# MLP up product by Strassen's seven products, hidden rows through DRAM, down product contraction-outermost

## The chip, the cores and the metric

The kernel runs on one core of a Trainium2 chip. The metric is the device time of one execution in microseconds; a profiled execution is taken beside it. Engines are named as in the profile: PE (TensorE, matmuls; PEld its weight loads), DVE (VectorE), ACT (ScalarE), POOL (GpSimd) and SP (SyncE, which issues the DMAs of this kernel). 

## The reference

One decoder layer over 1024 tokens with model width 1024. A normalised input is projected for three mixers (a gated convolution, a state-space scan, a windowed attention), which are gated, summed and projected back; then comes a cross-attention over 256 memory tokens, and then the MLP. What the change touches is the end:

```
h = h + CrossAttn(RMSNorm(h), RMSNorm(mem))       # ends with a product by w_xo, 1024 x 1024
u = RMSNorm(h)                                    # gain g_mlp per channel, 1/rms per token
h = h + relu(u @ w_mlp_up)**2 @ w_mlp_down        # 1024 -> 4096 -> 1024
```

All data are float32.

## The kernel before

Activations lie with channels on the 128 partitions and the 1024 tokens along the free side: a tile `ht[i]` is 128 channels x 1024 tokens, eight of them are the residual stream h.

Every product is made from split operands. A float32 tile is cut into a rounded part (`oh`, `wh`, a copy by ACT into the fp32r type) and the rest (`ol`, `wl`, a subtraction by DVE for activations, by POOL for weights). A product is then three matmuls, high x high, high x low, low x high, added up in PSUM. A matmul has 128 x 128 weights and 512 tokens. `gemm_ch` makes one output tile of 128 x 1024 in a pair of PSUM banks (pool `pg`, two such tiles): 6 matmuls for each 128 channels of contraction, so 48 for a contraction of 1024 and 24 for one of 512. Pool `pss` has four more banks, and the eight banks are then all used. `wslot` loads 128 x 1024 weights from DRAM by SP's queue into a staging tile (`wst`, two), and splits them by ACT (L155) and POOL (L156) into `wp` (three pairs).

The kernel is written in a tile framework: a tool orders the instructions by priorities and readiness and puts in the semaphores. Code inside `high_priority` (the weight loads) goes ahead of its place in the text. `after(n, fn)` lays small pieces of work n steps later between the matmuls of a product; `step()` counts these, and `drain()` runs what is left. `token_rstd` sums squares over channels by small matmuls and makes 1/rms per token; `spread` multiplies it into a diagonal and makes a tile of it, equal on all partitions, by four matmul records (`ps_bs`).

The end of the cross-attention: `project` (L1291) takes the heads in two halves of the contraction, each 8 outputs of 24 matmuls. DVE adds the result to `ht[i]` (L1298). In the second half, `done(i)` (L1317) also splits ht[i] with the gain g_mlp on it (ACT L1054, DVE L1055), squares it (ACT L1322) and sums the squares (POOL L1323). So the MLP multiplies un-normalised activations, and 1/rms comes in afterwards, because it is one number per token.

The MLP (L1334 to L1357) goes over eight blocks. A block makes four hidden tiles (`gemm_ch` with contraction 1024, 48 matmuls each). DVE takes the positive part times 1/rms out of PSUM (L1345), ACT squares (L1346) and rounds (L1051), DVE takes the difference (L1052). The four hidden tiles are then multiplied by `w_down` (contraction 512): eight outputs of 24 matmuls, each added by DVE to `ht` (L1355). In the last block the sums are stored (L1357).

The stage that follows the attention, `branch(load_split(...))` (L1069 to L1105), is the one place where a product's activations are loaded from DRAM and split (`yin`, L1076).

Of the kernel before, what the change touches and what calls it, by code (L numbers as in the profile page):

```python
# [9 lines left out]
F32 = mybir.dt.float32  # L10
F32R = mybir.dt.float32r
AF = mybir.ActivationFunctionType
# [43 lines left out]
def trunk_kernel(tc, w_io):  # L56
# [3 lines left out]
    with ctx:  # L60
# [26 lines left out]
        def after(n, fn):  # L87
            side.append((steps_done[0] + n, fn))
# [14 lines left out]
        def drain():  # L103
            while side:
                side.pop(0)[1]()
# [28 lines left out]
        d_v = dram.tile([NT, P, 256], F32, name="d_v")  # L134
        d_z = dram.tile([16, P, T], F32, name="d_z")
        d_cs = dram.tile([8, 32, P], F32, name="d_cs")
        d_bv = dram.tile([16, 384], F32, name="d_bv")
        d_skew = dram.tile([16, P * 385], F32, name="d_skew")

        def wslot(src, first=False, pool_=None, stage=None):  # L140
            with ExitStack() as e:
                if not first:
                    e.enter_context(tc.high_priority())
                st = (stage or wst).tile([P, 1024], F32, tag="ws", name="ws", bufs=2 if stage else None)
                if isinstance(src, list):
                    for n, part in enumerate(src):
                        nc.sync.dma_start(
                            st.rearrange("p (k n c) -> p k n c", k=2, n=2)[:, :, n, :],
                            part.rearrange("p (k c) -> p k c", c=256),
                        )  # L150
                else:
                    nc.sync.dma_start(st, src)
                wh = (pool_ or wp).tile([P, 1024], F32R, tag="wh", name="wh")
                wl = (pool_ or wp).tile([P, 1024], F32R, tag="wl", name="wl")
# [1030 lines left out]
        with ExitStack() as sc:  # L1185
# [102 lines left out]
                ):  # L1288
                    after(start + at, lambda fn=fn, args=args: fn(*args))

            def project(hh, parts, done):  # L1291
                for i2 in range(4):
                    wh, wl = wslot(w_io["w_xo"][hh, i2])
                    for j in range(2):
                        cols = lambda w, k: w[:, k * 256 + j * P:k * 256 + j * P + P]
                        ps = gemm_ch(lambda k: (cols(wh, k), cols(wl, k)), hi(parts), lo(parts), 4, T)
                        hv = ht[i2 * 2 + j]
                        dve.tensor_add(hv, hv, ps)  # L1298
                        done(i2 * 2 + j)

            parts0 = [pair(opb) for _ in range(4)]
            qT = queries(0)
            qT1 = queries(1)
# [7 lines left out]
            project(0, parts0, lambda i: None)  # L1311
            drain()
            both = q2.tile([P, 2, T], F32, tag="xqT", name="sq2")
            acc = both[:, 0, :]
            u3 = []

            def done(i):  # L1317
                u3.append(split(opc if i < 4 else opb, ht[i], C("g_mlp", i)))
                if i == 0:
                    act.activation(acc, ht[i], AF.Square)  # L1320
                else:
                    act.activation(both[:, 1, :], ht[i], AF.Square)  # L1322
                    pool.tensor_add(acc, acc, both[:, 1, :])  # L1323
            project(1, parts1, done)
            rb = xr.tile([P, T], F32, tag="acc", name="rb")
            dg = q2.tile([P, 2, T], F32, tag="xqT", name="hm_dg")
            r = []
            after(4, lambda: r.append(token_rstd(xr, acc, T, 1.0 / D, EPS, "hm")))
            after(6, lambda: spread(xr, r[0], T, "hm", rb, dg[:, 0, :]))
            up0 = gemm_ch(ch_slots(w_io["w_up"][0]), hi(u3), lo(u3), KT, T)  # L1330
            drain()


        with ExitStack() as sc:  # L1334
            ope = sc.enter_context(tc.tile_pool(name="ope", bufs=2))
            rt = sc.enter_context(tc.tile_pool(name="rt", bufs=2))
            n = 0
            for blk in range(8):
                parts = []
                for i in range(4):  # L1340
                    ps = up0
                    if blk or i:
                        ps = gemm_ch(ch_slots(w_io["w_up"][blk * 4 + i]), hi(u3), lo(u3), KT, T)
                    r = rt.tile([P, T], F32, tag="relu", name="relu")
                    dve.scalar_tensor_tensor(r, ps, 0.0, rb, ALU.max, ALU.mult)  # L1345
                    act.activation(r, r, AF.Square)  # L1346
                    parts.append(split(opa if n % 6 < 4 else ope, r))
                    n += 1
                for i2 in range(4):
                    wh, wl = wslot(w_io["w_down"][blk, i2])  # L1350
                    for j in range(2):
                        cols = lambda w, k: w[:, k * 256 + j * P:k * 256 + j * P + P]
                        ps = gemm_ch(lambda k: (cols(wh, k), cols(wl, k)), hi(parts), lo(parts), 4, T)
                        hv = ht[i2 * 2 + j]
                        dve.tensor_add(hv, hv, ps)  # L1355
                        if blk == 7:
                            nc.sync.dma_start(w_io["outT"][i2 * 2 + j], hv)  # L1357


# [105 lines left out]
```

## Time and profile before

| what | before |
|---|---|
| time, median of 3 runs | 2794.09 us (2794.03 to 2796.2) |
| time of the profiled execution | 2794.76 us |
| its span, first to last instruction | 2793.0 us |
| mean granted TensorE clock | 0.994 |
| PE / DVE / ACT / POOL busy, share of the span | 98% / 51% / 36% / 30% |
| matmul records | 12892 |
| moved by DMA | 267 MB, mean 96 GB/s |

A page of the profile gives the busy time of each engine, the same in 40 slices, the chain of work that ended last, and the costliest groups of instructions. A group's line has the line of the kernel, the engine, the operation, output<-inputs, partitions x elements, count, busy time, mean duration, and how long the engine stood idle before it and for whom. The trace behind it can be asked for a stretch, a line or a tile.

### The profile page before, as it was taken

To read this page: it belongs to the slowest core of one execution; us is meant where nothing else is said; L and a number is where in the kernel's file an instruction comes from. 1 tells how busy PE (TensorE), PEld (TensorE's weight loads), DVE (VectorE), ACT (ScalarE), POOL (GpSimd) and SP (SyncE) were. 2 spreads that over 40 slices of the span, in tenths; PEclk is the share of its full clock that TensorE was granted. 3 is DMA by queue.
4 is the path that set the end of the run, shared out by engine and by line. 5 is a ranking of instruction groups with operands and counts; after the bars stand their busy time and mean duration, and the time that the engine had idled before them with its cause. 6 is when DMAs were issued, how large, how long until landed. Compare 5 with 4: busy or idle time off the path is not lost. (4 is left out here: it accounts for less than half of the span.)

```text
span 2793.0 us, 31816 instructions
## 1 busy us (share of the span) xinstructions
PE 2737.7 (98%) x12892; PEld 2211.6 (79%) x12892; DVE 1430.1 (51%) x1610; ACT 1005.0 (36%) x1662; POOL 839.4 (30%) x376
## 2 busy tenths in 40 slices
PE   8899999999999999999899999999999999999999
PEld 6688878887787878765588778898778888888887
DVE  7578878759777876634414675223342222222222
ACT  6523321213565555556511352245432211122111
POOL 4622222201626252434242522420142222222221
PEclk9999999999999999999999999999999999999999
DMA  6552332321333233442444332310111111111111
GB/s 230 178 143 95 100 119 86 112 101 43 114 113 116 98 122 111 166 144 88 148 166 142 113 106 89 107 54 27 50 38 46 53 46 46 53 46 46 53 46 76
DMA packets 94515, 267.22 MB, mean 96 GB/s; under 512 B 9104, under 2 KB 34080, under 8 KB 93984
## 3 DMA queue, kind: packets, MB, share of 16 engines
q1 hardware_dynamic: 94368, 265.19, 28.6%
q8 instruction: 101, 1.65, 0.2%
q14 instruction: 46, 0.38, 0.0%
HBM read 210.47 MB, written 57.83 MB: 96 GB/s over the span
## 5 line engine op out<-in xcount | busy, mean ns | idle before, releaser
L156 POOL TENSOR_TENSOR wl<-ws,wh 128x1024 fp32r<-128x1024 f32 x200 | 500.7, 2506 | 1360.8 <-ACT wh L155 1330.9
L73 PE MATMUL ps_g<-oh,wh 128*128 128x512 f32 x1792 | 562.8, 395 | 4.1 <-ACT oh L1051 4.1
L73 PE MATMUL ps_g<-ol,wh 128*128 128x512 f32 x1792 | 555.6, 391 | 3.9 <-DVE ol L1052 3.4
L73 PE MATMUL ps_g<-oh,wl 128*128 128x512 f32 x1792 | 553.7, 390 | 0.0
L155 ACT CAST wh<-ws 128x1024 fp32r<-128x1024 f32 x200 | 209.7, 1049 | 869.6 <-PE ps_g L73 779.2
L332 DVE SCALAR_TENSOR_TENSOR tapy<-hin,cst,tapy 128x1024 f32<-128x1024 f32 x240 | 389.9, 1625 | 31.0 <-ACT tapy L327 24.7
L73 PEld LDWEIGHTS ps_g<-oh,wh 128*128 128x128 f32 x1792 | 335.6, 188 | 81.1 <-issue 7.1
L73 PEld LDWEIGHTS ps_g<-ol,wh 128*128 128x128 f32 x1792 | 335.8, 188 | 80.4 <-DVE ol L1052 9.7
L73 PEld LDWEIGHTS ps_g<-oh,wl 128*128 128x128 f32 x1792 | 336.9, 188 | 72.0
L73 PE MATMUL ps_g<-uh,wh 128*128 128x512 f32 x1008 | 330.6, 407 | 11.5 <-ACT uh L351 11.5
L73 PE MATMUL ps_g<-ul,wh 128*128 128x512 f32 x1008 | 324.4, 396 | 0.3 <-DVE ul L352 0.3
L73 PE MATMUL ps_g<-uh,wl 128*128 128x512 f32 x1008 | 315.7, 392 | 0.3 <-POOL wl L156 0.3
L73 PEld LDWEIGHTS ps_g<-ul,wh 128*128 128x128 f32 x1008 | 190.1, 189 | 50.0 <-issue 9.3
L73 PEld LDWEIGHTS ps_g<-uh,wl 128*128 128x128 f32 x1008 | 190.0, 189 | 41.7 <-POOL wl L156 1.2
L73 PEld LDWEIGHTS ps_g<-uh,wh 128*128 128x128 f32 x1008 | 178.9, 190 | 39.7 <-ACT uh L351 11.5
L1355 DVE TENSOR_TENSOR ht<-ht,ps_g 128x1024 f32<-128x1024 f32 x64 | 78.2, 1221 | 250.3 <-PE ps_g L73 250.3
L73 PE MATMUL ps_tm<-wh,uh 128*128 128x512 f32 x448 | 175.6, 392 | 0.0
L73 PE MATMUL ps_tm<-wh,ul 128*128 128x512 f32 x448 | 174.5, 389 | 0.0
L73 PE MATMUL ps_tm<-wl,uh 128*128 128x512 f32 x448 | 174.3, 389 | 0.0
L1345 DVE SCALAR_TENSOR_TENSOR relu<-ps_g,rb 128x1024 f32<-128x1024 f32 x32 | 39.2, 1225 | 221.8 <-PE ps_g L73 221.8
L170 POOL TENSOR_TENSOR wl<-ws,wh 128x1024 fp32r<-128x1024 f32 x28 | 74.9, 2685 | 218.5 <-ACT wh L169 218.5
L742 DVE SCALAR_TENSOR_TENSOR c4a<-c4v,cst,c4a 128x1023 f32<-128x1023 f32 (+2 forms) x72 | 98.7, 1370 | 32.0 <-ACT c4a L740 30.8
(341 smaller groups left out, 3417.3 us busy)
## 6 DMA issues: line engine op xcount, KB each, us to landing
ws<-w_ch SPq DMA_DIRECT2D x64, 512.0 KB, 3.5
csb<-d_cs SPq DMA_DIRECT2D x32, 512.0 KB, 4.0
gth<-d_th SPq DMA_DIRECT2D x32, 512.0 KB, 4.4
ws<-w_up SPq DMA_DIRECT2D x32, 512.0 KB, 3.3
ws<-w_down SPq DMA_DIRECT2D x32, 512.0 KB, 3.3
d_th<-gate_th SPq DMA_DIRECT2D x21, 512.0 KB, 5.1
ws<-w_xkv SPq DMA_DIRECT2D x32, 256.0 KB, 3.1
ws<-w_z SPq DMA_DIRECT2D x16, 512.0 KB, 3.3
```

The lines of the kernel that those rows point to most:

```text
L73: ins = nc.tensor.matmul(*a, **k)
L155: act.copy(wh, st)
L156: pool.tensor_sub(wl, st, wh.bitcast(F32))
L170: pool.tensor_sub(wl[:, :, c], s3, wh[:, :, c].bitcast(F32))
L332: dve.scalar_tensor_tensor(y, hin[:, j:j + T], w(j), y, ALU.mult, ALU.add)
L742: dve.scalar_tensor_tensor(a[:, s:], v[:, :T - s], C("c4_w", ct * 4 + 3 - s), a[:, s:], ALU.mult, ALU.add)
L1345: dve.scalar_tensor_tensor(r, ps, 0.0, rb, ALU.max, ALU.mult)
L1355: dve.tensor_add(hv, hv, ps)
```

## The change

In the projection's second half, 1/rms of the cross-attention's norm (already known) is spread over the partitions and multiplied into the MLP's input together with the gain. The outputs are made in the order 0, 4, 1, 5, 2, 6, 3, 7, so that each step has one tile of the upper and one of the lower half of the contraction. With tokens cut in two halves, the input is a 2 x 2 block matrix, and DVE makes the seven moving operands of Strassen's scheme (Winograd's form) from it: x11, x21, x22, t1 to t4, four tiles each, every one split in high and low part (`slice_of`). They fill the pools `opc`, `opb`, `opd` and the place of `ht` itself; h goes to DRAM (`d_h`).

The up product takes hidden tiles in 16 pairs. DVE makes the sums of weight blocks (s1, s2, s3 and one more), ACT and POOL split seven stationary operands per pair, PE makes seven products of 12 matmuls, each in one bank of `pss`, and DVE combines the results, takes relu and square in one operation, and SP stores them (`d_r`). ACT copies the first product out of PSUM.

The down product makes four output tiles at a time, in all eight PSUM banks, with the hidden rows outermost: each hidden tile is loaded from `d_r`, split, and multiplied into four outputs (24 matmuls); after 32 hidden tiles the outputs are multiplied by a per-token factor, added to h (loaded from `d_h`) and stored. This is done twice. The factor is the square of the ratio of the MLP norm's 1/rms to the one used on the input, made during the up product (`factor`).

```diff
-        def wslot(src, first=False, pool_=None, stage=None):
+        def wslot(src, first=False, pool_=None, stage=None, tags=("wh", "wl")):
...
+        def slice_of(name, src):
+            pool_, tag = next(spares)
+            t = pool_.tile([P, 2, 512], F32R, tag=tag, name="blk")
+            act.copy(t[:, 0, :], src)
+            dve.tensor_sub(t[:, 1, :], src, t[:, 0, :].bitcast(F32))
+            blocks.setdefault(name, []).append(t)
...
+            after(0, lambda: spread(xr, rx[0], T, "hx", rbx, dg))
+            for kp in range(4):
+                if kp % 2 == 0:
+                    slots = [wslot(w_io["w_xo"][1, kp // 2 + 2 * q]) for q in range(2)]
+                vs = []
+                for q in range(2):
+                    i = kp + 4 * q
+                    project(parts1, slots[q], i // 2, kp % 2)
+                    nc.sync.dma_start(d_h[i], ht[i])
+                    v = tp.tile([P, T], F32, tag="v", name="v")
+                    dve.scalar_tensor_tensor(v, ht[i], C("g_mlp", i), rbx, ALU.mult, ALU.mult)
...
+                        act.activation(sq, ht[i], AF.Square)
+                        pool.tensor_add(acc, acc, sq)
+                    lo_, hi_ = v[:, :512], v[:, 512:]
+                    if q == 0:
+                        slice_of("x11", lo_)
+                        t1 = tp.tile([P, 512], F32, tag="t1", name="t1", bufs=1)
+                        dve.tensor_sub(t1, hi_, lo_)
+                        slice_of("t1", t1)
+                t2, t3 = (tp.tile([P, 512], F32, tag="t", name="t") for _ in range(2))
+                b12, (b21, b22) = vs[0][:, 512:], (vs[1][:, :512], vs[1][:, 512:])
+                dve.tensor_sub(t2, b22, t1)
+                slice_of("t2", t2)
+                slice_of("x21", b21)
+                slice_of("x22", b22)
+                dve.tensor_sub(t3, b22, b12)
+                slice_of("t3", t3)
+                dve.tensor_sub(t2, b21, t2)
+                slice_of("t4", t2)
...
+            ORDER = (6, 1, 5, 7, 2, 3, 4)
+            for pr in range(16):
+                order = ORDER if pr else (1, 5, 6, 2, 3, 7, 4)
+                with tc.high_priority():
...
+                        w = (wst if q else mp).tile([P, 1024], F32, tag="ws", name="ws", bufs=2)
+                        nc.sync.dma_start(w, w_io["w_up"][pr * 2 + q])
...
+                    dve.tensor_add(s1, a21, a22)
+                    dve.tensor_sub(s2, s1, a11)
+                    dve.tensor_sub(s3, a11, a21)
...
+                            st[j] = stationary(srcs[j])
...
+                def square(o):
+                    dve.scalar_tensor_tensor(o, o, 0.0, o, ALU.max, ALU.mult)
+
+                for j in order:
+                    ps = banks[j] = pss.tile([P, 512], F32, tag="s", name="ps_up")
+                    for k in range(4):
+                        x = blocks[names[j]][k]
+                        wh, wl = (st[j][:, h, k * P:(k + 1) * P] for h in range(2))
+                        pe.matmul(ps, wh, x[:, 0, :], start=k == 0, stop=False)
+                        pe.matmul(ps, wh, x[:, 1, :], start=False, stop=False)
+                        pe.matmul(ps, wl, x[:, 0, :], start=False, stop=k == 3)
...
+                    if j == 1:
+                        act.copy(p1, ps)
+                    if j in (1, 6) and {1, 6} <= seen:
+                        dve.tensor_add(u2, p1, banks[6])
+                    if j in (5, 6) and {5, 6} <= seen:
+                        dve.tensor_add(u5, u2, banks[5])
+                    if j == 7:
+                        dve.tensor_add(u2, u2, ps)
+                        o = rb_[:, 512:]
+                        dve.tensor_add(o, u2, banks[5])
+                        square(o)
...
+                        nc.sync.dma_start(d_r[pr * 2 + 1], rb_)
...
+            for hf in range(2):
...
+                    for k in range(4):
+                        n = blk * 4 + k
+                        r = opc.tile([P, T], F32, tag="ol", name="r_in")
+                        nc.sync.dma_start(r, d_r[n])
...
+                        xh, xl = split(opb, r)
+                        for q in range(4):
...
+                            for h in range(2):
+                                sl = slice(h * 512, h * 512 + 512)
+                                pe.matmul(outs[q][h], wh, xh[:, sl], start=n == 0, stop=False)
+                                pe.matmul(outs[q][h], wh, xl[:, sl], start=False, stop=False)
+                                pe.matmul(outs[q][h], wl, xh[:, sl], start=False, stop=n == 31)
...
+                                    dve.tensor_mul(o[:, sl], outs[q][h], f[0][:, sl])
+                                    if hf:
+                                        dve.tensor_add(o[:, sl], o[:, sl], hs[q][:, sl])
+                                        nc.sync.dma_start(w_io["outT"][i][:, sl], o[:, sl])
...
+                                    pool.tensor_add(o, o, hs[q])
```

A stationary operand of an up pair (`stationary`) is split by an ACT copy and a POOL subtraction of 512 elements each, and there are ten buffers for them (three pairs of `wp`, four of `opa`).

## Rows read from the trace of the kernel before

**Rows 1.** The page: busy time and share of the span of each engine; the busy tenths of PE in 40 slices; the granted clock in tenths.

```profile
PE 2737.7 (98%) x12892; PEld 2211.6 (79%) x12892; DVE 1430.1 (51%) x1610; ACT 1005.0 (36%) x1662; POOL 839.4 (30%) x376
...
PE   8899999999999999999899999999999999999999
...
PEclk9999999999999999999999999999999999999999
```

**Rows 2.** Busy time by stretch: the second half of the projection, and the MLP from its first to its last matmul. Columns: stretch, its length, busy us (count) of PE, PEld, DVE, ACT, POOL, granted clock, DMA share, GB/s.

```profile
2035.20:2078.75 43.55, 43.55 (x194) 36.04 (x193) 20.27 (x16) 18.99 (x19) 25.53 (x10) 1.00 0.15 49
2078.75:2788.20 709.45, 707.00 (x3093) 578.28 (x3091) 160.58 (x137) 137.41 (x132) 152.58 (x64) 1.00 0.15 50
```

**Rows 3.** The chain of work that ended last, over one block of the MLP: start us, us, what.

```profile
2132.28 82.82 PE ps_g L73 x364
...
2215.13 1.24 DVE relu L1345
...
2216.38 1.07 ACT relu L1346
...
2217.48 1.06 ACT oh L1051
...
2218.56 1.24 DVE ol L1052
...
2219.84 83.54 PE ps_g L73 x364
```

**Rows 4.** Timeline of PE: two neighbouring records of the steady stretch, two behind a seam, and three at the seam. Start us, us, engine, line, operation, output<-inputs, count of matmuls in the record.

```profile
2126.46 0.62 PE L73 MATMUL ps_g<-ol,wh 128*128 128x512 f32 x2
2126.91 0.62 PE L73 MATMUL ps_g<-oh,wl 128*128 128x512 f32 x2
...
2217.26 0.63 PE L73 MATMUL ps_g<-oh,wl 128*128 128x512 f32 x2
2217.73 0.63 PE L73 MATMUL ps_g<-oh,wh 128*128 128x512 f32 x2
...
2219.11 0.61 PE L73 MATMUL ps_g<-oh,wh 128*128 128x512 f32 x2
2219.84 0.73 PE L73 MATMUL ps_g<-ol,wh 128*128 128x512 f32 x2
2220.41 0.39 PE L73 MATMUL ps_g<-oh,wl 128*128 128x512 f32 x1
```

**Rows 5.** Durations of single operations, by line and by tile: ns min/median/max, first and last start, shape. The first two are of the projection stage; then half-width operations of DVE and ACT; then POOL's weight difference at full and another POOL operation at half width.

```profile
L1298 DVE TENSOR_TENSOR ht<-ht,ps_g x16: 1220/1222/1222, 1964.7 to 2078.9; 128x1024 f32<-128x1024 f32 x16
L1055 DVE SCALAR_TENSOR_TENSOR ol<-ht,cst,oh x16: 1274/1716/3078, 1752.9 to 2081.4; 128x1024 fp32r<-128x1024 f32 x16
L1264 DVE TENSOR_TENSOR xp<-xp,xrd x16: 681/692/694, 1887.0 to 2018.6; 128x512 f32<-128x512 f32 x16
L1281 ACT CAST oh<-ps_xo x16: 567/587/592, 1904.8 to 2034.0; 128x512 fp32r<-128x512 f32 x16
L156 POOL TENSOR_TENSOR wl<-ws,wh x200: 2349/2402/5788, 10.1 to 2755.6; 128x1024 fp32r<-128x1024 f32 x100
L797 POOL TENSOR_TENSOR xtok<-xtok,cst x32: 1039/1896/2025, 708.1 to 1157.1; 128x512 f32<-128x512 f32 x32
```

**Rows 6.** The layer norm of the merge stage, where DVE and POOL work on SBUF at the same time: one record of eight DVE operations (timeline), one of five of POOL (timeline), all eight and all seven of them by line, and, for DVE operations that read PSUM, the additions of the MLP (by line).

```profile
1572.50 18.02 DVE L1130 TENSOR_TENSOR yconv<-yconv,ln_mean 128x1024 f32<-128x1024 f32 x8
1576.03 16.77 POOL L1136 TENSOR_TENSOR ln_acc<-ln_acc,lnsq 128x1024 f32<-128x1024 f32 x5 [4.54 <-ACT lnsq L1135]
...
L1130 DVE TENSOR_TENSOR yconv<-yconv,ln_mean x8: 1212/2319/3435, 1572.5 to 1587.1; 128x1024 f32<-128x1024 f32 x8
...
L1136 POOL TENSOR_TENSOR ln_acc<-ln_acc,lnsq x7: 3266/3275/3364, 1576.0 to 1596.3; 128x1024 f32<-128x1024 f32 x7
...
L1355 DVE TENSOR_TENSOR ht<-ht,ps_g x64: 1220/1221/1223, 2133.5 to 2788.2; 128x1024 f32<-128x1024 f32 x64
```

**Rows 7.** Groups of PE's small matmuls at the MLP's norm: count, busy us, mean ns, idle time before.

```profile
L73 PE MATMUL ps_bs<-hm_dg,mat 128*128 128x512 f32 x4 | 2.0, 619 | 0.0
L73 PE MATMUL ps_st<-mat,sq 128*128 128x1 f32 x16 | 1.9, 251 | 1.1 <-POOL sq L1323 1.1
```

**Rows 8.** The entry of the merge stage, whose activations are loaded from DRAM: SP's queue (a load of the new stage, a store of the earlier one), then a load, ACT's cast of it and the matmul that waited (timeline), and the busy time by stretch there (columns as in rows 2).

```profile
1351.27 0.46 SPq L1076 DMA_DIRECT2D yin<-d_yb  x1
...
1361.51 0.43 SPq L1014 DMA_DIRECT2D d_yc<-oT  x1
...
1379.79 1.10 SPq L1076 DMA_DIRECT2D yin<-d_yb  x2
...
1383.39 1.99 ACT L1051 CAST oh<-yin 128x1024 fp32r<-128x1024 f32 x2 [4.12 <-DMA yin<-d_yb]
...
1384.49 1.22 PE L73 MATMUL ps_g<-oh,wh 128*128 128x512 f32 x2 [4.08 <-ACT oh L1051]
...
1382.60:1389.40 6.80, 4.88 (x11) 3.38 (x12) 2.36 (x2) 1.99 (x2) 0.00 (x0) 0.50 0.94 333
```

**Rows 9.** The end: the last addition, the last store (timeline), and the time of the stores to landing.

```profile
2788.18 1.22 DVE L1355 TENSOR_TENSOR ht<-ht,ps_g 128x1024 f32<-128x1024 f32 x1 [4.32 <-PE ps_g L73]
2789.43 0.33 SPq L1357 DMA_DIRECT2D outT<-ht  x1
...
DMA to landing us min/median/max: 2.6/2.6/2.6
```

More of the change, by code (lines that the diff above doesn't have):

```diff
@@ L152, in wslot @@
                     nc.sync.dma_start(st, src)
-                wh = (pool_ or wp).tile([P, 1024], F32R, tag="wh", name="wh")
-                wl = (pool_ or wp).tile([P, 1024], F32R, tag="wl", name="wl")
+                wh = (pool_ or wp).tile([P, 1024], F32R, tag=tags[0], name="wh")
+                wl = (pool_ or wp).tile([P, 1024], F32R, tag=tags[1], name="wl")
                 act.copy(wh, st)
@@ L1289, in attend, with project @@
                     after(start + at, lambda fn=fn, args=args: fn(*args))
[L1291 to L1299, printed above, removed]
+            def project(parts, slot, i2, j):
+                wh, wl = last_slot[0] = slot
+                cols = lambda w, k: w[:, k * 256 + j * P:k * 256 + j * P + P]
+                ps = gemm_ch(lambda k: (cols(wh, k), cols(wl, k)), hi(parts), lo(parts), 4, T)
+                hv = ht[i2 * 2 + j]
+                dve.tensor_add(hv, hv, ps)
+            last_slot = [None]
             parts0 = [pair(opb) for _ in range(4)]
@@ L1310, in trunk_kernel @@
             attend(3, qT3, parts1[2:], 15)
-            project(0, parts0, lambda i: None)
+            for i2 in range(4):
+                project(parts0, wslot(w_io["w_xo"][0, i2]), i2, 0)
+                project(parts0, last_slot[0], i2, 1)
             drain()
[L1313 to L1320, printed above, removed]
-                else:
-                    act.activation(both[:, 1, :], ht[i], AF.Square)
-                    pool.tensor_add(acc, acc, both[:, 1, :])
@@ L1324, in trunk_kernel, with spare @@
[L1324 to L1330, printed above, removed]
+        def spare():
+            for pool_, tags, n in ((opc, ("oh", "ol"), 4), (opb, ("oh", "ol"), 4), (opd, ("sl",), 3)):
+                for tag in tags:
+                    for _ in range(n):
+                        yield pool_, tag
+            for i in (0, 4, 1, 5, 2, 6, 3, 7):
+                yield hp, f"ht{i}"
+            yield opd, "sl"
@@ L1331, in trunk_kernel @@
             drain()
         with ExitStack() as sc:
[L1335 to L1357, printed above, removed]
@@ new lines, in trunk_kernel @@
+            dp = sc.enter_context(tc.tile_pool(name="down", bufs=2))
+            for hf in range(2):
+                outs = []
+                for q in range(4):
+                    if q < 2:
+                        ps = pg.tile([P, T], F32, tag="g", name="ps_d")
+                        outs.append([ps[:, :512], ps[:, 512:]])
+                    else:
+                        outs.append([pss.tile([P, 512], F32, tag="s", name="ps_d2") for h in range(2)])
+                hs = []
+                for blk in range(8):
+                    slots = []
+                    for i2 in range(2):
+                        if blk % 2:
+                            slots.append(wslot(w_io["w_down"][blk, hf * 2 + i2], pool_=opa, tags=("oh", "ol")))
+                        else:
+                            slots.append(wslot(w_io["w_down"][blk, hf * 2 + i2]))
+                    for k in range(4):
+                        n = blk * 4 + k
+                        r = opc.tile([P, T], F32, tag="ol", name="r_in")
+                        nc.sync.dma_start(r, d_r[n])
+                        if 20 <= n < 24:
+                            hs.append(opd.tile([P, T], F32, tag="sl", name="hv"))
+                            nc.sync.dma_start(hs[-1], d_h[hf * 4 + n - 20])
+                        xh, xl = split(opb, r)
+                        for q in range(4):
+                            wh, wl = (w[:, k * 256 + q % 2 * P:k * 256 + q % 2 * P + P] for w in slots[q // 2])
+                            for h in range(2):
[3 more added lines that the diff above has]
+                                pe.matmul(outs[q][h], wl, xh[:, sl], start=False, stop=n == 31)
+                            step()
+                            if n == 31:
+                                i = hf * 4 + q
+                                o = dp.tile([P, T], F32, tag="o", name="o")
+                                for h in range(2):
+                                    sl = slice(h * 512, h * 512 + 512)
+                                    dve.tensor_mul(o[:, sl], outs[q][h], f[0][:, sl])
+                                    if hf:
+                                        dve.tensor_add(o[:, sl], o[:, sl], hs[q][:, sl])
+                                        nc.sync.dma_start(w_io["outT"][i][:, sl], o[:, sl])
+                                if not hf:
+                                    pool.tensor_add(o, o, hs[q])
+                                    nc.sync.dma_start(w_io["outT"][i], o)
```

73 lines of the change are left out of this document (added).

## Prediction

> **What bounds the kernel now.** I read the page first: PE is busy 98% of the span at full granted clock, DVE 51%, POOL 30% [rows 1]. Only matmul work taken away, or PE idle time removed, can shorten this kernel; any new wait of PE lengthens it. Then the busy times by stretch for the part that the change touches [rows 2]: the last projection of the cross-attention runs 43.55 us, and the MLP 709.45 us to the last matmul, both with PE busy almost throughout and DVE, ACT and POOL at a quarter to a half. The chain of waits [rows 3] shows once per block of four hidden rows 2215.13 to 2219.84: relu, square, cast and difference, 4.7 us in the chain. A reader is tempted to book 8 x 4.7 = 38 us for it. The timeline of PE [rows 4] corrects that: the matmul pair before the seam starts at 2219.11, the next at 2219.84 instead of 2219.56, and takes 0.57 instead of 0.45 us. PE works on the first three of the four hidden tiles while the fourth goes through ACT and DVE, so a seam costs 0.4 us, 3.2 us in all.
>
> The same timeline gives the price of a matmul: 2126.46 to 2126.91 is 0.453 us for two, 226.7 ns each. Behind some seams it is a little more (2217.26 to 2217.73, 0.47 for two). 3072 matmuls at 226.7 ns are 696.4 us; the MLP's 709.45 leave 13.0 for the norm's small matmuls (3.9, [rows 7]), the 3.2 of seams, about 1 of the wait at the norm, and some 5 us of wider spacing.
>
> **The change, part by part.** The profiled execution took 2794.76 us, 1.76 more than its span and 0.7 more than the median; I work on its times and subtract from the median of 2794.09.
>
> *Fewer products.* Up: 32 tiles x 48 matmuls = 1536 become 16 pairs x 7 products x 12 = 1344. Down stays 2 x 32 x 24 = 1536. So 192 x 226.7 ns = -43.5 us. Each matmul has its own weight load now and has it afterwards, and the moving side stays 512 wide, so I keep the spacing. The Trainium skill ("TensorE: Matmul & The Clock Gate", Back-to-back issue gap and the step on spacing before it) gives 215.7 ns for 512 columns at the full clock; by it the saving would be 41.4 us. The row differs, and the row decides.
>
> *Wider spacing.* If it held for all 2880 matmuls at the 0.47 per pair of [rows 4], it would cost up to 2880 x 8 ns = 23 us; if it went, it would give back 5. I take no change.
>
> *Seams of the blocks go*: -3.2 us.
>
> *One spread more.* The x-norm factor is now spread at the start of the projection and a quotient later in the up stage: two spreads instead of one, four more matmul records on PE, +2.0 us [rows 7].
>
> *The projection stage.* This is the large cost. Today each of its outputs gives DVE an addition (1.22) and a difference (1.28 alone, median 1.72) in 5.44 us of PE [rows 5]. Afterwards two outputs (10.9 us of PE) give DVE two additions, two scalings (2 x 1.28) and eleven half-width operations: one x11 difference, t1 and its difference, and t2, t3, t4, x21, x22 with theirs. A half-width operation is 0.69 us [rows 5], so 2.44 + 2.56 + 7.59 = 12.6 us. DVE alone already passes PE. On top comes POOL. In the layer norm of the merge stage, eight SBUF-only DVE operations that take 1.21 each alone took 18.02 us beside four of POOL's sums [rows 6]: (18.0 - 9.7)/4 = 2.1 us of DVE for one 2.4 us POOL operation, and POOL's sums grew to 3.3. DVE operations that read PSUM are untouched (1220 to 1223 ns, [rows 6]). In the changed stage all eleven half-width operations and the scalings are of the kind that suffers, and POOL has two sums per two outputs. So a step costs DVE 12.6 + 4.2 = 16.8 us against 10.9.
>
> The Trainium skill ("SBUF — State Buffer", Two separate sides) says more sharply that the port pair which VectorE shares with GpSimd is an exclusive lock held for the whole instruction, and the loser blocks fully. By it a POOL sum costs DVE 2.4, and the stall below would come out 8 x 0.3 = 2.4 us larger; the row's 2.1 is what I use.
>
> PE can run ahead of DVE by two outputs (two PSUM tiles), so DVE's lateness reaches PE. The first up product needs the x11 slice of the fourth step. Until then: first output 5.4; step one 12.6 + 2.1 = 14.7 (the first output has no sum); steps two and three 33.6; of step four an addition, a scaling, a sum and a difference, 5.3; the two weight splits of the second half of w_xo on POOL, 4.2; the first pair's weight work (three half-width sums on DVE, about three half-width POOL operations at 1.04), 5. Sum 68.2; less about 3 because neighbouring DVE operations overlap by some 0.07 us. PE without stall wants the slice after 201 x 0.2267 = 45.6. The stall is 19.6 us. The third product then wants t2 of step four: 8.0 us of DVE and ACT behind x11, against 24 matmuls = 5.4, 2.5 more. I take +22. Below, if every POOL operation fell beside a PSUM addition or a DVE pause, the sum is 68.2 - 3 less all eight POOL prices and three stationaries (20) = 45: no stall. Above, 30, with PE at half clock behind its gaps [rows 8].
>
> *The up pairs themselves.* Per pair PE has 84 x 0.2267 = 19.0 us. DVE has 15 half-width operations, 10.4 us; ACT eight copies at 0.59; POOL seven at 1.04 to 1.2 (half of 2.40), 8.4 us. Ten stationaries are alive, so weights are ready products ahead, and a PSUM bank is wanted again two products (5.4 us) after the result that frees it. I take 0; the bound above is a rival below.
>
> *Through DRAM.* Stores and loads move 0.5 MB of hidden rows and 0.25 MB of weights per 5.44 us in the down stage, 145 GB/s against 50 now [rows 2]; near the middle of the kernel the queues moved 333 [rows 8]. Four load tiles and four split pairs run ahead. Costs nothing in the steady state. On SP the loads stand behind stores that wait for DVE, the last two behind the last square. At the entry of the merge stage the same thing (a split from DRAM) made PE wait 4.08 us, and the granted clock was 0.50 (1.2 GHz) for 6.8 us after PE had stood still [rows 8]. But there SP issued a first load at 1351.27, ahead of a store of the earlier stage at 1361.51 [rows 8], so the queue's order is not that of the text. From 0 to 10 for this seam; I take +2.
>
> *The end.* Now: last matmul, addition 1.22, store 2.6 [rows 9]. After: the second half ends with four outputs 1.36 us of PE apart, each with four half-width DVE operations, 2.76. DVE starts on the first 4.6 us before PE ends and works 16 x 0.69 = 11.0 us: it ends 6.4 us behind PE instead of 1.2. +5 us, 4 to 7.
>
> *Sum*: -43.5 - 3.2 + 2.0 + 22 + 0 + 2 + 5 = -15.7; 2794.1 - 15.7 = **2778 us**.
>
> **Rivals.**
>
> *The projection stage stays covered* (DVE keeps up, POOL falls beside PSUM work; seam free). For it: DVE's waits come only where the two engines start together, and today's differences often ran at 1.27. Against it: the eight operations of [rows 6]. Without 22 and 2: 2754 us.
>
> *The four PSUM banks bind in the up stage: slower.* DVE carries weight sums, combinations and squares in one queue. If in two of the seven products of a pair an operation that frees a bank stands behind one POOL operation (1.2 us) more than its slack, PE waits 2.4 us per pair, 38 us: 2817. It decides from 15.7/16 = 1.0 us per pair on. For it: DVE and POOL together hold 10.4 + 8.4 = 18.8 of 19.0 us if they never overlap. Against it: seven of the fifteen DVE operations read PSUM, and the two-product slack is 5.4 us.
>
> *Every bound at its upper part, no stall per pair* (projection 30, DRAM seam 10): 2794, no change.
>
> **Chances.** The forecast, 2765 to 2788: 0.48. Covered stage, below 2765: 0.20. No gain, 2788 to 2800: 0.12. Slower: 0.20. 0.2% is 5.6 us, which is about what a measurement here tells from no change: faster, below 2788.5, 0.68; same 0.12; slower 0.20. The range for 8 in 10 leaves out 1 in 10 on each side: 2753 to 2808; the likeliest case alone spans 2765 to 2788.
>
> **What would show it.** PE idle in the projection stage, released by DVE, in gaps of 2 to 6 us and some 20 in all, with DVE over nine tenths busy and its SBUF operations at two or three times 0.69 us; PEclk halved for short stretches there. PE records of the up stage at 226 to 232 ns with no idle time. 2880 matmuls of the MLP. A gap under 3 us where the down stage begins. DVE as the last engine, 5 to 7 us behind PE. I am wrong if PE waits in every pair of the up stage (the banks), if loads of hidden rows release PE in the down stage, or if the projection stage shows no wait of PE.

## Result and the profile after

The changed kernel takes 2799.81 us in the median against 2794.3 us for the kernel before, beside which it was run: ratio 1.0018, 95% interval 1.0011 to 1.0025. A gain of 16 us was forecast and 5 us were lost. The profiled execution's span went from 2793.0 to 2798.1 us, and the account below is made on these two traces.

The page of the kernel after, lines that answer to [rows 1]:

```profile
PE 2702.5 (97%) x12704; PEld 2181.8 (78%) x12704; DVE 1637.3 (59%) x1858; ACT 1058.9 (38%) x1780; POOL 937.4 (34%) x460
...
PE   8899999999999999999899999999977999999998
...
PEclk9999999999999999999999999999997999999999
```

PE is busy 35 us less than before and the span is 5 us longer, so some 40 us of idle time are new. PE's digits have their hole at slices 30 and 31, the end of the projection and the first up pairs, and the clock's at slice 31. The busy time by stretch of the kernel after cuts this place finer (columns as in [rows 2]; projection's second half, gap, first up pairs, the other up pairs, first down half, the seam of the two halves, second half):

```profile
2035.50:2090.50 55.00, 49.01 (x197) 38.31 (x195) 48.15 (x45) 21.84 (x32) 19.53 (x8) 0.94 0.21 81
2090.50:2113.50 23.00, 0.01 (x2) 0.01 (x1) 19.02 (x20) 7.72 (x13) 8.25 (x4) 0.55 0.22 80
2113.50:2150.00 36.50, 31.38 (x109) 23.53 (x110) 23.66 (x31) 11.19 (x19) 20.97 (x15) 0.77 0.22 73
2150.00:2434.60 284.60, 284.60 (x1258) 235.64 (x1257) 183.03 (x217) 74.01 (x117) 139.89 (x100) 1.00 0.32 116
2434.60:2611.30 176.70, 176.70 (x781) 146.17 (x779) 57.40 (x42) 53.23 (x51) 46.11 (x19) 1.00 0.52 175
2611.30:2620.00 8.70, 4.32 (x12) 2.82 (x12) 4.13 (x5) 1.05 (x1) 8.70 (x5) 0.80 0.70 248
2620.00:2789.00 169.00, 169.00 (x747) 139.68 (x745) 42.74 (x35) 38.88 (x37) 23.62 (x10) 1.00 0.36 119
```

The account, by the 226.7 ns of [rows 4]. Before, from 2035.20 to 2788.20 are 753.0 us: 43.5 for the projection's 192 matmuls, 696.4 for the MLP's 3072, and 13.1 in which PE did not stream. After, from 2035.4 to 2789.1 are 753.7: 43.5, then 652.9 for 2880, and 57.3. Of these 57.3, 57.1 lie in four places: the projection (55.1 - 43.5 = 11.6), the gap (23.0), the first pairs (36.5 less 89 matmuls at 226.7 ns = 16.3), the seam of the down halves (6.2). So +44.2 eats the saving of 43.5; the end adds 4.2 and a stage that begins 0.2 later the rest of 5.1.

What PE waited for in the kernel after, from 2030 to 2800 us, the four longest (who waits, on what, us in total, times, longest):

```profile
PE ps_up L73 <- ACT st L1407: 23.0, 1, 23.0
PE ps_g L73 <- DVE ht L1298: 6.0, 3, 3.7
PE ps_d L73 <- DVE o L1521: 4.4, 2, 3.7
PE ps_bs L73 <- DVE f_dg L260: 3.6, 1, 3.6
```

The first line names ACT, but ACT's copy takes 0.6 us. The chain of the kernel after tells what is behind it, from 2080 to 2130 us (start, us, what):

```profile
2084.53 2.78 DVE t L1371
...
2092.51 2.75 DVE t L1377
...
2097.58 0.68 DVE blk L1337
...
2108.24 0.70 DVE blk L1337
...
2109.08 3.71 DMA ws<-w_up
...
2112.82 0.63 ACT st L1407
...
2113.52 4.73 POOL st L1408 x3
...
2122.01 8.22 POOL st L1408 x6
```

DVE has x11 of step four at 2098.26 and its last slice at 2108.9. Only then does SP load the second of the first pair's two weight tiles, for this one lies in the memory of the projection's scratch pool, which has just closed (SP's queue, timeline):

```profile
2058.87 0.33 SPq L1418 DMA_DIRECT2D ws<-w_up  x1
...
2109.08 11.30 SPq L1418 DMA_DIRECT2D ws<-w_up  x4
```

Then POOL's stationaries set the pace. And each of POOL's sums holds up one of DVE's operations; DVE and POOL in the kernel after (timeline):

```profile
2078.22 2.74 DVE L1367 TENSOR_TENSOR t<-v 128x512 f32<-128x512 f32 x1
...
2084.53 2.77 DVE L1371 TENSOR_TENSOR t<-v,t 128x512 f32<-128x512 f32 x1
2087.22 0.68 DVE L1375 TENSOR_TENSOR t<-v 128x512 f32<-128x512 f32 x1
...
2101.22 2.72 DVE L1371 TENSOR_TENSOR t<-v,t 128x512 f32<-128x512 f32 x1
```

```profile
2077.62 2.80 POOL L1362 TENSOR_TENSOR h_acc<-h_acc,sq 128x1024 f32<-128x1024 f32 x1 [6.71 <-ACT sq L1361]
2083.32 3.43 POOL L1362 TENSOR_TENSOR h_acc<-h_acc,sq 128x1024 f32<-128x1024 f32 x1 [2.91 <-ACT sq L1361]
...
2100.62 2.78 POOL L1362 TENSOR_TENSOR h_acc<-h_acc,sq 128x1024 f32<-128x1024 f32 x1 [5.91 <-ACT sq L1361]
```

A half-width operation that takes 0.68 alone takes 2.7 to 2.8, and each time it ends 0.54 to 0.55 us after POOL's sum: 2080.96 after 2080.42, 2087.30 after 2086.75, 2103.94 after 2103.40. It reads as if DVE stood still until POOL is done. All seven sums in the trace do this to one operation each: the seven take 19.4 us instead of 7 x 0.68 = 4.8, so 14.6 us of DVE are lost.

### The profile page after: what moved, and what is told of

It reads as the page before. It is cut to its first block, busy times and chain, and to the rows that moved or that the text cites. A ratio compares the mean times of both kernels' runs of the same rounds, so it can differ in the third digit from the quotient of the medians.

```text
span 2798.1 us, 32362 instructions
## 1 busy us (share of the span) xinstructions
PE 2702.5 (97%) x12704; PEld 2181.8 (78%) x12704; DVE 1637.3 (59%) x1858; ACT 1058.9 (38%) x1780; POOL 937.4 (34%) x460
## 4 chain that ended last, share of the span: by engine, by line
PE 79%; DVE 10%; issue 4%; POOL 2%; DMA 2%; ACT 2%; SPq 0%; DVEq 0%; ACTq 0%; POOLq 0%
PE ps_g L73 34%; PE ps_d L73 12%; PE ps_tm L73 12%; PE ps_up L73 10%; DVE tapy L334 3%; PE ps_yd L73 2%; DVE c4a L744 1%; POOL wl L158 1%; PE ps_lg L73 1%; PE ps_xl L73 1%; PE ps_xo L73 1%; PE ps_pt L77 1%; PE ps_yo L73 1%; PE ps_stt L73 1%; ACT lg L977 1%
## 5 line engine op out<-in xcount | busy, mean ns | idle before, releaser
L158 POOL TENSOR_TENSOR wl<-ws,wh 128x1024 fp32r<-128x1024 f32 x168 | 427.7, 2550 | 1053.2 <-ACT wh L157 993.0
L73 PE MATMUL ps_up<-blk,st 128*128 128x512 f32 x1344 | 311.7, 394 | 24.5 <-ACT st L1407 23.0
L73 PEld LDWEIGHTS ps_up<-blk,st 128*128 128x128 f32 x1344 | 255.8, 191 | 80.1 <-ACT st L1407 23.4
L73 PE MATMUL ps_g<-oh,wh 128*128 128x512 f32 x768 | 247.5, 404 | 10.1 <-DVE ht L1298 6.0
L73 PE MATMUL ps_g<-ol,wh 128*128 128x512 f32 x768 | 239.4, 393 | 2.5 <-DVE ol L1054 2.4
L73 PE MATMUL ps_g<-oh,wl 128*128 128x512 f32 x768 | 238.1, 391 | 0.0
L73 PE MATMUL ps_d<-oh,wh 128*128 128x512 f32 x512 | 199.9, 390 | 4.4 <-DVE o L1521 4.4
L73 PE MATMUL ps_d<-ol,wh 128*128 128x512 f32 x512 | 199.7, 390 | 0.0
L73 PE MATMUL ps_d<-oh,wl 128*128 128x512 f32 x512 | 199.6, 390 | 0.0
L73 PEld LDWEIGHTS ps_g<-oh,wh 128*128 128x128 f32 x768 | 144.0, 190 | 47.0 <-issue 8.1
```

What stands on the lines that cost most here:

```text
L73: ins = nc.tensor.matmul(*a, **k)
```

## Experiments

The kernel before ran beside each of them, so times are given with the ratio to it; "less than after" is the difference of the medians from 2799.81, which was measured at another time. The kernel before itself differed by up to 1.3 us between these times (2793.29 to 2794.54), so differences of about that size are not told apart. A diff is against the kernel after, where nothing else is said.

**1. The shared memory.** Theory A: the gap is the weight load that waits for the scratch pool. Theory B: it is the work of DVE and POOL, which hold each other up.

```diff
-                        w = (wst if q else mp).tile([P, 1024], F32, tag="ws", name="ws", bufs=2)
+                        w = (wst if q or not pr else mp).tile([P, 1024], F32, tag="ws", name="ws", bufs=2)
...
+                        s0 = [opa.tile([P, 2, 512], F32, tag="ol", name="s0") for _ in range(2)]
+                        s1, s2, s3 = s0[0][:, 0, :], s0[0][:, 1, :], s0[1][:, 0, :]
```

> Edit: for the first pair only, both weight tiles are loaded into the two old staging tiles, and the three weight sums lie in tiles of the projection's operands, so nothing that the first product needs lies in the memory that the projection stage's scratch tiles occupied. Theory (shared memory): in the trace after, SP issued the first pair's second weight load at 2109.08, behind the projection stage's last DVE operation at 2108.9, and PE waited 23.0 us. With the load free, PE starts when the x11 slice of the fourth step is split, which was 2098.3: the gap falls from 23.0 to about 8 us, and the kernel by 10 to 15 us, to 2785 to 2790. Rival (DVE's order): PE has to wait for DVE in any case, because the weight sums and POOL's weight splits stand behind the slices: the gap shrinks by less than 5 us, or what it loses comes back as waits in the first two pairs, and the time stays within 4 us of 2800.

2799.56 us, ratio 1.0019 (1.0010 to 1.0029): no gain. PE's waits in this run:

```profile
PE ps_bs L73 <- DVE f_dg L260: 13.2, 1, 13.2
PE ps_up L73 <- ACT blk L1336: 12.6, 1, 12.6
```

The wait of 23.0 is gone; a new one of 12.6 and 9.6 more on `f_dg` (13.2 instead of 3.6) have about its length. DVE now does the first pair's weights earlier and the slices of step four later; the last one ends at 2118.1 instead of 2108.9. The wait that a trace names was real and yet worth nothing: A falls.

**2. POOL's sums of squares left out.** The second norm then rests on the squares of one tile alone.

```diff
-                        pool.tensor_add(acc, acc, sq)
```

> Edit: POOL's seven sums of squares in the projection stage are left out (so the second norm uses the squares of one tile alone, and the output is not the reference's); all else as in the changed kernel. Theory of the prediction (DVE and POOL hold each other up): each sum costs DVE about 2.1 us; the stage's DVE work, which ended at 2108.9, ends 12 to 15 us earlier, PE waits less in the projection and the first up product starts 12 to 15 us earlier; the kernel falls by 12 to 18 us. Rival (count of DVE operations alone, or ACT's casts that DVE waits for): DVE ends within 4 us of 2108.9 and the time falls by less than 5.

2783.14 us, ratio 0.9965 (0.9952 to 0.9978): 16.7 less than after, for seven sums. PE's waits: none in the projection, 16.9 at the first stationary. DVE's last slice ends at 2092.5 instead of 2108.9, 16.4 us earlier, where 12 to 15 were expected. One of the operations that a sum had held up each time, in the kernel after and in this run (by line; ns min/median/max):

```profile
L1371 DVE TENSOR_TENSOR t<-v,t x4: 2723/2770/2774, 2050.8 to 2101.2; 128x512 f32<-128x512 f32 x4
...
L1370 DVE TENSOR_TENSOR t<-v,t x4: 691/693/693, 2049.9 to 2086.8; 128x512 f32<-128x512 f32 x4
```

So the sums are the cause of the stretching: B holds for the projection.

**3. Four output tiles in the down product.**

```diff
-            dp = sc.enter_context(tc.tile_pool(name="down", bufs=2))
+            dp = sc.enter_context(tc.tile_pool(name="down", bufs=4))
```

> Edit: four instead of two output tiles in the down stage. Theory: the 3.7 us wait between the two halves of the down product (and the half clock behind it, 6.2 us in all) is that of DVE for an output tile whose store has not landed, which holds back a PSUM bank. With four tiles no store is waited for; the gap goes and the kernel falls by 6 us, to 2794. Rival: PE waits because DVE has eight PSUM reads and two differences to do beside POOL's additions; then the gap stays at 2 us or more and the time falls by less than 3.

2791.96 us, ratio 0.9991 (0.9982 to 1.0001): 7.8 less than after, where 6 were expected. In the kernel after the seam of the halves reads so (timeline):

```profile
2609.38 5.68 POOL L1526 TENSOR_TENSOR o<-o,hv 128x1024 f32<-128x1024 f32 x2
...
2611.80 3.62 SPq L1527 DMA_DIRECT2D outT<-o  x2
...
2614.51 1.29 DVE L1521 TENSOR_TENSOR o<-ps_d,rb 128x512 f32<-128x512 f32 x2 [1.65 <-DMA outT<-o]
...
2615.25 0.79 PE L73 MATMUL ps_d<-oh,wh 128*128 128x512 f32 x1 [3.73 <-DVE o L1521]
```

The third output may take its tile when the first one's store has landed; DVE waits for that, and PE for the banks that DVE has not emptied. With four tiles PE has no wait there, and the rival falls.

**4. The norm's factor later.**

```diff
-            after(8, factor)
+            after(60, factor)
```

> Edit: the factor of the second norm is made 60 steps into the up product instead of 8. Theory: its chain of small DVE operations stands in DVE's queue behind the first pairs' backlog, PE waits 3.6 us for the diagonal, and its matmuls of 3.8 us run at a granted clock of 0.5; later, with DVE idle a third of the time, the wait goes and the four records take 2.0. The kernel falls by 5 to 9 us, to 2791 to 2795. Rival: the first pairs are bound by POOL's weight splits, and PE only waits for them instead: less than 3 us.

2795.66 us, ratio 1.0006 (0.9997 to 1.0016): 4.2 less than after, just short of the theory's 5 and over the rival's 3. The wait for f_dg fell from 3.6 to 2.0 only, but the four spread matmuls took 1.95 us instead of 3.75, at full clock.

**5. Matmuls without use in the gap,** to see whether the half clock is the cause.

```diff
+        for i in range(100):
+            pe.matmul(idle[:, :512], blocks["x11"][0][:, 0, :P], blocks["x11"][0][:, 0, :], start=True, stop=True)
```

> Edit: 100 extra matmuls of 512 columns, whose result nobody reads, stand on PE between the projection and the first up product, so that PE is not idle in the 23.0 us gap (100 x 0.2267 = 22.7 us). Nothing else differs. Theory (half clock): in the changed kernel the granted clock was 0.5 for 27.3 us from 2092.8 on and for two short stretches behind it, and about 27 up matmuls were 0.427 instead of 0.227 us apart and the spread's records 1.9 us longer: 5 to 7 us of the loss is the clock, and the kernel falls by that, to 2793 to 2795. Rival (POOL's chain): in those pairs PE waits for POOL's weight splits in any case, so a faster PE only waits: the time stays within 2 us of 2799.8.

2798.97 us, ratio 1.0014 (1.0005 to 1.0024): 0.8 less than after, not told apart from nothing: the rival held. The granted clock was full from the gap until 2127.5, and PE waited instead:

```profile
PE ps_bs L73 <- DVE f_dg L260: 3.6, 1, 3.6
PE ps_up L73 <- DVE u L1462: 3.0, 1, 3.0
PE ps_up L73 <- ACT st L1411: 1.4, 1, 1.4
PE ps_up L73 <- POOL st L1412: 1.1, 1, 1.1
```

A slow PE hid the waits for DVE and POOL; in this stretch the clock is a companion of the loss, not its cause. The spread's matmuls took 3.75 us in this run too, so for them it tells nothing; experiment 4 does.

**6. The new down product alone,** with projection and up product as before (1/rms is multiplied in with the relu, hidden rows go through DRAM). The diff is against the kernel before.

```diff
-            for blk in range(8):
...
+            for n in range(32):
+                ps = gemm_ch(ch_slots(w_io["w_up"][n]), hi(u3), lo(u3), KT, T) if n else up0
...
+                nc.sync.dma_start(d_r[n], r)
```

> Edit: the down half of the change alone. The projection stage and the up products are those of the kernel before (32 plain hidden tiles, 48 matmuls each), the hidden tiles go through DRAM, the down product is the changed one (hidden rows outermost, eight banks), and the residual is still in SBUF, so that the end is one addition per half output and no factor. Theory (the saving is Strassen's 192 matmuls, the loss lies in the projection stage and the first pairs): the seams of the blocks (3.2 us) and the wider spacing (5 us) go, the half seam costs 0 to 3, the time is 2785 to 2792. Rival (the trip through DRAM or the order of the down product costs something of its own): 2796 or more, with loads of hidden rows as releasers of PE.

2788.75 us, ratio 0.9980 (0.9971 to 0.9989): 5.8 less than the kernel before beside it (2794.54), inside the theory's range. In the down product PE waited 0.8 and 0.4 us in all.

**7. The sums of squares moved** to the up pairs 2 to 9, where h is read from `d_h`; nothing is left out.

```diff
-                        pool.tensor_add(acc, acc, sq)
...
+                if 2 <= pr < 10:
+                    hq = opa.tile([P, T], F32, tag="ol", name="hq")
+                    nc.sync.dma_start(hq, d_h[pr - 2])
...
+                        pool.tensor_add(acc, acc, hq)
+                if pr == 11:
+                    factor()
```

> Edit: the sum of squares for the second norm is taken out of the projection stage; h is read back from DRAM one tile per pair in the pairs 2 to 9 of the up product, squared by ACT and summed by POOL there, and the factor is made in pair 11. Nothing is left out. Theory (DVE and POOL hold each other up in the projection stage): the 16.7 us that leaving the sums out gave are kept, since POOL is busy half the time and DVE two thirds in the up product, and the late factor adds 4: the kernel falls by 17 to 22 us against the changed one, to 2778 to 2783. Rival (the up product has no slack for more POOL work): PE waits in the pairs 2 to 9, and half or more is given back: 2788 or more.

2777.11 us, ratio 0.9938 (0.9923 to 0.9952): 22.7 less than after, a little more than the theory's 17 to 22. That is 6.0 more than leaving the sums out. Two more things have left the first stretch here: the factor's chain, which gave 4.2 in experiment 4, and ACT's squares, which no run moved alone. PE's waits:

```profile
PE ps_up L73 <- ACT st L1400: 16.9, 1, 16.9
PE ps_d L73 <- DVE o L1524: 4.9, 2, 3.7
PE ps_up L73 <- POOL st L1401: 0.7, 1, 0.7
```

From 2130 to 2400 us PE is busy without a break in this run: the same sums cost nothing in the pairs 2 to 9.

**8. Experiments 7 and 1 together.**

> Edit: as e8_stats, and also the first pair's weights and sums kept out of the projection's scratch memory as in e1_alias. Theory: with POOL relieved, what bound the start in e1_alias (weight splits and sums of squares between DVE's slices) is smaller, PE's wait for the shared memory (16.9 us without the sums of squares) turns into one for the last slices of 8 us or less, and the kernel falls by 5 to 10 us more than e8_stats. Rival: the queue of DVE decides the start alone; the same work in another order gives the same time, as in e1_alias, within 3 us of e8_stats.

2774.51 us, ratio 0.9929 (0.9914 to 0.9944): 2.6 less than in 7, inside the rival's 3. The wait of 16.9 became 8.6 for a slice of x11 and 5.9 for a stationary.

**9 and 10. All that helped.** Experiment 7 with four output tiles; then also 1, and POOL's additions in two of the last four outputs.

```diff
-                                    if hf:
+                                    if hf and q > 1:
                                         dve.tensor_add(o[:, sl], o[:, sl], hs[q][:, sl])
...
-                                if not hf:
+                                if not hf or q < 2:
                                     pool.tensor_add(o, o, hs[q])
```

> The sums of squares moved to the up pairs 2 to 9, as before, and four output tiles instead of two in the down product; nothing is left out. Theory (the two losses lie in different stages and add): 2777.1 less the 7.8 that four output tiles gave by themselves, so 2768 to 2771, and no wait at the half seam of the down product. Rival (with the spread's work moved, the down product already meets its half seam at another time or the output queue binds anyway): less than 3 us below 2777.1, and the wait for DVE's o stays.

> All that helped, together: the sums of squares in the up pairs 2 to 9, the first pair's weight tiles in memory of their own, four output tiles, and the additions of the last rows shared by DVE and POOL; nothing is left out. Theory (the parts add): 2774.5 less 7.8 for the output tiles, less 1 to 3 for the end, where DVE ended 5.9 us behind PE: 2763 to 2766. Rival (POOL's additions of 512 columns at the end hold DVE up by the shared port, so that the end gains nothing or loses): 2767 to 2771, with PE's last matmul at least 9 us ahead of the end of the span.

2767.35 us, ratio 0.9904 (0.9889 to 0.9919), and 2766.06, ratio 0.9899 (0.9882 to 0.9915). The first came out 9.8 below experiment 7, a little more than the theory's 6 to 9. The second gained 1.3 on it, too little to tell apart. By its time it lies between the theory (to 2766) and the rival (from 2767); by the trace the end gained nothing, as the rival had it: from the end of PE's last matmul to the end of the span are 9.0 us in the first and 8.8 in the second, where the rival asked for 9. DVE at the end of the second (timeline):

```profile
2752.58 3.84 DVE L1528 TENSOR_TENSOR o<-ps_d,rb 128x512 f32<-128x512 f32 x6 [15.44 <-PE ps_d L73]
2756.34 3.47 DVE L1530 TENSOR_TENSOR o<-o,hv 128x512 f32<-128x512 f32 x2
2759.73 1.27 DVE L1528 TENSOR_TENSOR o<-ps_d,rb 128x512 f32<-128x512 f32 x2
2760.93 1.28 DVE L1530 TENSOR_TENSOR o<-o,hv 128x512 f32<-128x512 f32 x2
```

Six operations that read PSUM take 3.84 us, 0.64 each, most of it beside POOL. Two that use SBUF alone take 3.47 there and 1.28 without POOL. Both versions beat the two kernels: 26 and 27 us under the kernel before beside them, 32 and 34 under after.

**11 and 12. Amount or place?** 14.5 to 17 us of wait were left at the first up product. If DVE's work only comes too late, it helps to make x11 and t1 first. (Four of the scalings are made in two halves here, so DVE has four operations more, not the same number as expected.) The second run shares the memory again.

```diff
-                for q in range(2):
-                    i = kp + 4 * q
...
+            for i in range(8):
...
+                if i < 4:
...
+                    slice_of("x11", b11)
+                    dve.tensor_sub(t1[i], b12[i], b11)
+                    slice_of("t1", t1[i])
```

> The outputs of the projection in the order 0 to 7 instead of 0, 4, 1, 5, ...: x11 and t1 are then made in the first half of the stage, t2, x21, x22, t3, t4 in the second; the sums of squares in the up pairs 2 to 9, the first pair's weight tiles in memory of their own, four output tiles; nothing is left out, and DVE and POOL do the same number of operations. Theory (the amount of work fits, its place does not: the first two products want only what the first half of the stage makes): the 14.5 us that PE waited at the up product's start fall to 6 to 9, 2757 to 2761. Rival (the amount of DVE and POOL work in the stage is the bound, and the wait only moves to the third product): 2763 to 2767.

> The same order of outputs, but with the first pair's weight tiles again in memory that the projection stage has used. Theory (with DVE's last operation of the stage no earlier, the first weight load waits for it as before): one wait of 12 to 17 us for the first stationary operand, 2764 to 2768, at least 4 us over the version with memory of its own. Rival (the shared memory costs nothing, as in the two runs before): within 2.6 us of it.

2770.86 us, ratio 0.9918 (0.9903 to 0.9933), and 2771.28, ratio 0.9919 (0.9902 to 0.9935). The theory falls: the first is 4.8 above experiment 10, the second 3.9 above experiment 9, each with the same memory, and worse even than the rival had it. The shared memory again costs nothing that can be told apart (0.4), though PE's one wait for it reads 21.1 us. Busy time by stretch of the first of the two:

```profile
2055.00:2080.00 25.00, 25.00 (x112) 20.71 (x111) 22.64 (x30) 9.25 (x17) 3.00 (x3) 1.00 0.25 100
2080.00:2097.00 17.00, 9.05 (x35) 6.27 (x33) 17.00 (x18) 5.69 (x10) 8.43 (x6) 0.86 0.20 70
2097.00:2130.00 33.00, 23.68 (x89) 18.16 (x90) 28.37 (x31) 11.24 (x20) 20.29 (x13) 0.86 0.29 96
```

DVE (the third busy time) is at 91% while PE still streams, and at 100% when PE begins to wait. So this other order did not help, and the busy time speaks for the amount of DVE's work, stretched by POOL's stationaries, as the rest of the loss. That it is the amount was not shown by a run with less of it.

## Why the prediction was wrong

The sign was wrong, by one term that was half its size and one that was missing. Term by term, on the traces:

- *Fewer products, -43.5*: right. The up stage after 2150 and each down half run at 226.7 ns without a wait. 2880 matmuls of the MLP are in the trace (1344 `ps_up`, 1536 `ps_d`).
- *Wider spacing, no change*: wrong in the good direction. It went, and gave back about 5 us by the account. Experiment 6, with the old up product, was 5.8 us faster than before, by this and the seams of the blocks together.
- *Up pairs, 0*, and the rival of the four banks: right for the steady part; from 2150 to 2434.6 PE is busy 284.60 of 284.60 us. The rival would have had PE wait in every pair. The kernel came out slower, as this rival had it, but by other waits.
- *Through DRAM, +2*: 0. PE goes from the last up matmul to the first down matmul without a gap; the loads of hidden rows release nothing.
- *The end, +5*: 4.2. DVE ends 5.7 us behind PE, where 6.4 was worked out.
- *The half seam*: no term at all, 6.2 in the trace and 7.8 by experiment 3. The prediction looked at the seam into the down stage and at its end, and not at the place between, where two `o` tiles wait for their stores.
- *The projection stage, "I take +22"*: the failed step; in the same account it measured 44, twice as much. Its price was right: it put a POOL sum at 2.1 us of DVE by [rows 6], and the stretched operations above lost 2.0 to 2.1 each, 14.6 for all seven. Leaving the seven out gave 16.7 (experiment 2), 2 us more than that, which stay unexplained. It put the x11 slice of step four 65.2 us after the stage's start, at 2100.6, and the slice ended at 2098.26. That is near, but in part by luck: the 65.2 hold 5 us for the first pair's weights, and in the trace all but one stationary of that work came later; without the 5 the working says 60.2 against 62.9. And there it stopped. "The first pair's weight work" was booked at 5 us, before that slice, and after it only "2.5 more". In the trace, 15.2 us lie between the slice and the first up matmul. PE then loses 16.3 us more until 2150, of which some 6 are the norm's small matmuls and spread that the working had. The engines that were late at the stage's end had the rest of the last step, two pairs' sums and stationaries and the norm's factor still to do, one after the other. Projection, gap and first pairs lost 50.9 us. The working had 22 + 2.0 for the spread + 3.9 + 1 for the norm, 28.9. Take the 6.9 for spread and norm off both, and the 22 of the working stand against 44.0.

The sum of the misses: 22.0 (projection and first pairs) + 6.2 (half seam) - 5 (spacing) - 2 (DRAM) - 0.8 (end) = 20.4; between -15.7 and +5.1 are 20.8. None of the three signs by which the prediction said it would be wrong appeared: it failed at a place for which it had named no sign.

The third rival, "every bound at its upper part", came near the time (2794) by another sum: its 30 for the projection is still 14 short of the 44, and its 10 for the DRAM seam did not come.

Of the two rules of the Trainium skill in the prediction, "TensorE: Matmul & The Clock Gate" (Back-to-back issue gap and the step on spacing before it) gives 215.7 ns for matmuls of 512 columns issued back to back; the trace after has 226.7 again. "SBUF — State Buffer" (Two separate sides) has the loser of the shared port blocked for the whole instruction. The timeline agrees: DVE's operation ends 0.54 to 0.55 us behind POOL's sum each time. What DVE loses, 2.0 to 2.1 us, is less than the sum's length of 2.8 or 3.4, since its operation begins 0.6 or 1.2 us later than the sum.

What stays open: how the last 14.5 to 17 us of waiting at the first up product divide between DVE's own operations and its standing still for POOL. No run took the slices off DVE, or the stationaries off POOL. Nor did a run take the loss of the first stretch apart in full: the sums and the factor are tried, the rest is read from the traces.

## What to carry to other kernels

When a change takes matmuls away by giving other engines more work, book DVE's and POOL's SBUF work of a stage as one serial sum, and follow it until PE runs steadily again, not only to the first operand that is late. Work that is not needed soon belongs where PE does not wait for the engine that does it: the same sums cost some 17 us in the projection and nothing in the up pairs. A single long wait in the list need not be worth its length: taking away the memory that it waited for moved it to the next operand, three times.

## What the hardware showed unexpectedly

The granted clock of the kernel after was 0.50 (1.2 GHz) for 27.3 us, but PE worked for 6 of them only and stood idle for the others (by stretch, columns as in [rows 2]):

```profile
2092.80:2113.50 20.70, 0.01 (x1) 0.01 (x1) 16.72 (x18) 7.21 (x12) 5.95 (x3) 0.50 0.21 76
2113.50:2120.10 6.60, 5.95 (x13) 4.26 (x14) 4.20 (x5) 1.55 (x4) 5.96 (x4) 0.50 0.23 81
```

Matmuls that kept the clock full there gained 0.8 us, not told apart from nothing, as PE then waited for the engines that feed it (experiment 5). And PE's spacing went with what the other engines did: with the old up product and the old down product some matmuls came 235 ns apart, with the new down product, beside the old up product or the new one, nearly all came at 226.7 in the steady parts; which of the operations beside it widened the spacing was not tried.
